# Layer 0's last MLP group added in HBM, one input combination kept in HBM, projection weights in pairs: a hybrid two-layer trunk on one Trainium2 core

## The chip, the core and the metric

The kernel runs on one core of one Trainium2 chip. Its time is the device time of one execution in microseconds (us); of the kernel before, three runs have a median of 2133.31 us (2131.84 to 2133.79). One further execution was recorded by the hardware profiler; all rows shown below come from it.

The engines are named as in the profile: PE is the matrix engine (PEld its weight loads), DVE the vector engine, ACT the scalar engine, POOL the GpSimd engine, SP the sync engine, which here only issues DMAs. L12 is line 12 of the kernel before.

## What is computed

A residual stream `x` of 1024 positions by 1024 features passes through two layers. Each layer adds a mixer and then an MLP. All data are float32.

```python
for layer in range(2):
    h = rms_norm(x, norm_mix[layer])
    if layer == 0: y_mix, xq = rglru_group(h, ...)   # gated linear recurrence
    else:          y_mix, xq = fox_group(h, ...)     # causal attention with forgetting
    y_mem = memory_group(xq, mem, ...)               # cross-attention into 256 memory tokens
    x = x + concat([y_mix, y_mem]) @ w_out[layer]
    x = x + square(relu(rms_norm(x, norm_mlp[layer]) @ w_mlp_in[layer])) @ w_mlp_out[layer]
```

`memory_group` also needs keys and values of the memory tokens: `rms_norm(mem, g_mem) @ w_kv`.

## The kernel before

The stream is held transposed in HBM (`xs`, in the trace `xspill`): eight feature blocks `m` of 128 partitions, each with 1024 positions that are worked on in two halves `h` of 512. Every float32 operand of a matmul is split into a high and a low part (`split`, `split_sb`: ACT writes the high part, DVE subtracts to get the low one), and every product is made of three matmuls (`t3`): high by high, high by low, low by high. Weights are split in the same way in `_wpart` (L316 on ACT, L317 on DVE or POOL), from four raw buffers `wr` into a ring of three `wh`/`wl` pairs. The list `plan` gives the order of the weights; `wnext` splits up to two entries ahead of the one that it returns. Raw weights are loaded by DMAs that SP issues in order (L312).

All working tiles of 128x512 are drawn from one pool of 86 slots, `F` for float32 and `R` for split parts. `get` takes the slot that was freed longest ago; the new user then waits until the last use of the old one has ended, a DMA out of it included.

**The MLP.** One Strassen-Winograd step is applied: per group `g` of eight, `mlp_z` makes the seven products of the first matrix, each of 24 matmuls of 128x512, and `mlp_out` the seven of the second. The left operands are combinations of weight blocks: for the third of a unit's seven, called S2, `_wunit` makes sums of raw blocks in place (L355 to L360), on POOL, or on DVE where the unit's `dve` is set. The right operands of `mlp_z` are five combinations of the input, `t1`, `t2`, `t3`, `t4` and `b22`, and the half 0 parts `b11` and `b21`, all split once by `xquad` and `xsplit` and held in slots for all eight groups. Each product's result goes from PSUM into slots (`copies`, L1028 on ACT; `plus`, L1033 on DVE), and in groups 0 to 6 `send` adds the sixteen finished tiles of a group into `xs` by DMAs that POOL issues with an add at the destination (L1172). In group 7 of both layers `keep` and `end` instead bring `xs` into the sums (L1192 on POOL for a quarter, by DMA with add into the tile at L1195 for a half, `acc` for the last quarter), and `sink` (L1174 on) writes the finished tile, to `xs` in layer 0 and to the output in layer 1. In layer 0 `sink` also makes the squares of every tile (L438), adds them up (L444) and splits the half 0 tiles into the next mixer's input (L468, L469).

**From layer 0 to layer 1.** `kv(1)` prepares the memory tokens (splits at L587 and L590, squares at L593, their sum at L597 on POOL) during `mlp_z` of group 7, and makes the memory's keys and values right behind the MLP; then come `norm_fin(0)`, the query projection `xq_proj(0, 1)`, the first memory attention and the forgetting attention, and `norm_split` for half 1, which loads half 1 from `xs` and splits it.

**Layer 1's MLP.** The first products of groups 0 to 3 are made early, during the mixer (`mlp_park`); group 0's four result tiles stay in slots, those of groups 1 to 3 go to HBM and are read back by `mlp_back` in the middle of `mlp_out` of the group before.

**Layer 1's output projection** uses `wout1m` and `wout1x`, each as eight entries of 512 columns, one for each output block `m`. Each set is used twice, once for each half; the second time its split parts are loaded back from HBM by POOL's DMAs (L332).

Within these functions the instructions are written out as a list; the tile framework keeps data dependences and orders each engine's instructions by a simulated schedule, so an instruction may run ahead of one that was written before it on the same engine.

Of the kernel before, what the change touches and what calls it, by code (L numbers as in the profile page):

```python
# [175 lines left out]
class Builder:  # L176
# [4 lines left out]
    def __init__(self, ctx, tc, ins, out):  # L181
# [36 lines left out]
        self.parked = {}  # L218
        self.stp = {}
# [246 lines left out]
    def split(self, xt, g, n=H):  # L466
        hi, lo = self.R.get(), self.R.get()
        self.last_hi = self.nc.scalar.activation(hi[:, :n], xt, AF.Copy, scale=g)  # L468
        self.nc.vector.scalar_tensor_tensor(lo[:, :n], xt, g, hi[:, :n].bitcast(F32), ALU.mult, ALU.subtract)  # L469
        return hi, lo  # L470
# [42 lines left out]
    def norm_split(self, h, g, src, stats):  # L513
        xs = self.xg[h] = []
        for k in range(8):
# [3 lines left out]
            xs.append(self.split(x[:, :H], self.pc(g, k)))  # L519
            self.F.put(x)  # L520
# [368 lines left out]
    def outproj(self, h, ks, src, dst, gain, last, banks=("pj",)):  # L889
        nc = self.nc  # L890
        for m in range(8):
            x = self.load_x(m, h, src)
            wh, wl = self.wnext()
            ps = self.psum(banks[m % len(banks)])
            terms = []
            for i, k in enumerate(ks):
                c = slice(i * P, (i + 1) * P)
                terms += self.t3(wh[:, c], wl[:, c], *(self.ymix[h][k] if k < 4 else self.ymem[h][k - 4]))
# [91 lines left out]
    def xsplit(self, key):  # L990
        n = slice(0, H)
        for q, f, g in self.later.pop(key, ()):
            self.tp[key][q] = self.split_sb(f[:, n]) if g is None else self.split(f[:, n], g)
            self.F.put(f)

# [6 lines left out]
    def plan_mlp(self, l, parked, wait):  # L1002
        for g in wait:
            self.plan_unit("w1", 8 * l + g, Unit.ALL[1:2])
        for g in range(8):
            u = self.plan_unit("w1", 8 * l + g, Unit.ALL[2:] if g in parked + wait else Unit.ALL)
            u.dve = g == 0
            self.plan_unit("w2", 8 * l + g)
# [64 lines left out]
    def mlp_z(self, l, g, hook):  # L1073
        nc = self.nc
        V = nc.vector
        n = slice(0, H)
        xp = dict(self.tp, b11=self.xg[0][0::2], b21=self.xg[0][1::2])
# [4 lines left out]
        def run(banks, key, start, done):  # L1082
            hook(key)
            yield from self.product(banks, xp[key], start, done)
            if g == 7:
# [67 lines left out]
    def mlp_out(self, l, g, mid):  # L1153
        nc = self.nc
        V, G = nc.vector, nc.gpsimd
        n = slice(0, H)
        hp = self.hp
        seen = set()
# [15 lines left out]

        def sink(f, q, a, b):
            x, dm = f[:, n], 2 * q + a
            nc.sync.dma_start((self.out if l else self.xs)[dm, :, b * H:(b + 1) * H], x)
            if l == 0:
                self.sqacc(1 if b in seen else 0, b, x, V if b == 0 and a == 1 else None)
                seen.add(b)  # L1180
                if b == 0:
                    self.xg[0][dm] = self.split(x, self.pc("gmix1", dm))
            self.F.put(f)

        def keep(a, b):
            dst = []

            def first(q, ps):
                self.copies(dst)(q, ps)
                if g == 7 and a == b == 0:  # L1190
                    f = self.acc.pop(0)
                    G.tensor_tensor(dst[q][:, n], dst[q][:, n], f[:, n], ALU.add)  # L1192
                    self.F.put(f)
                elif g == 7:
                    nc.gpsimd.dma_start(dst[q][:, n], self.xs[2 * q + a, :, b * H:(b + 1) * H], accum_op=ALU.add)  # L1195

            def then(q, ps):
                self.plus(dst[q], ps)
                (sink if g == 7 else send)(dst[q], q, a, b)
# [3 lines left out]
        def end(q, ps):  # L1203
            if g == 7:
# [15 lines left out]
        acc = [self.load_x(2 * q, 1, self.xs) for q in range(4)] if g == 7 else None  # L1220
# [5 lines left out]
    def mlp(self, l, wait, nxt=None):  # L1226
# [9 lines left out]
        def hook7(key):  # L1236
            if key in ("t2", "b22") and nxt is not None:
                advance(nxt)
            if key == "t1":
# [551 lines left out]
```

## Time and profile before

| what | value |
|---|---|
| median of three runs | 2133.31 us |
| profiled execution, its own time | 2132.37 us |
| profiled execution, span from first to last instruction | 2130.7 us |
| PE busy | 2071.5 us, 97% of the span, 10466 matmuls |
| DVE busy | 1663.3 us, 78% |
| ACT busy | 1141.9 us, 54% |
| POOL busy | 864.0 us, 41% |
| mean granted PE clock | 0.988 |
| moved by DMA | 298.44 MB, 140 GB/s over the span |

The MLP of layer 0 ends at about 985 us of the span and that of layer 1 at its end. In a table of windows, each row gives a stretch of the span, its length, then busy time and number of instructions of each engine, the granted PE clock (1.00 is full), the mean busy share of the 16 DMA engines and what they moved. In a list of waits a row names the waiting instruction, what released it, the total of the waits, their number and the longest. In a list of groups, a row gives line, engine, operation, tiles and shapes and the count, then the busy time in us and the mean of one instruction in ns, then the idle time of the engine ahead of it.

### The profile page before, as it was taken

How to read it: one execution, taken by the hardware profiler on the slowest of the kernel's cores; microseconds unless marked ns; L12 is line 12 of the kernel's file. 1: busy time of each engine (PE TensorE's matmuls, PEld its weight loads, DVE VectorE, ACT ScalarE, POOL GpSimd, SP SyncE). 2: the span in 40 equal slices, each digit the busy share in tenths (PEclk: the TensorE clock that was granted, in tenths of full speed). 3: DMA queues.
4: the chain of work that ended last, by engine and by line, in shares of the span. 5: the costliest groups of instructions: out<-in, count | busy, mean ns of one | idle time of the engine just before them, and what ended most of it. 6: DMA issues, size and time to landing. Idle time of an engine off the chain costs nothing. (4 is left out here: it accounts for less than half of the span.)

```text
span 2130.7 us, 30055 instructions
## 1 busy us (share of the span) xinstructions
PE 2071.5 (97%) x10466; PEld 1727.4 (81%) x10466; DVE 1663.3 (78%) x2708; ACT 1141.9 (54%) x2160; POOL 864.0 (41%) x844
## 2 busy tenths in 40 slices
PE   9999999999999999988999999999999999999998
PEld 8898878878778778767998998777777877787786
DVE  7988698877877877887677778776787768868777
ACT  6755655544454454555555646566544554445443
POOL 2222321535535525545342333422054645445444
PEclk8999999999999999989999999999999999999999
DMA  5422452546545635627768446934546675364474
GB/s 180 140 77 93 135 184 94 101 89 128 101 97 119 111 87 119 156 86 199 276 218 290 133 138 214 299 122 129 161 99 139 138 150 101 85 140 94 89 173 119
DMA packets 126392, 298.44 MB, mean 140 GB/s; under 512 B 14176, under 2 KB 16288, under 8 KB 126240
## 3 DMA queue, kind: packets, MB, share of 16 engines
q1 hardware_dynamic: 82464, 208.36, 29.4%
q0 software_dynamic: 43776, 88.17, 23.2%
q8 instruction: 82, 1.34, 0.3%
q14 instruction: 70, 0.57, 0.1%
HBM read 187.32 MB, written 109.15 MB: 139 GB/s over the span
## 5 line engine op out<-in xcount | busy, mean ns | idle before, releaser
L317 DVE TENSOR_TENSOR wl<-wr,wh 128x1024 fp32r<-128x1024 f32 (+2 forms) x362 | 441.2, 1229 | 108.5 <-ACT wh L316 104.1
L1017 PE MATMUL pspt<-r,wh 128*128 128x512 f32 x1536 | 485.1, 396 | 7.2 <-DVE r L477 2.6
L1172 POOL DMA_DIRECT2D xspill<-f x224 | 284.7, 1963 | 287.5 <-DVE f L1033 284.1
L316 ACT ACTIVATE wh<-wr 128x1024 fp32r<-128x1024 f32 (+3 forms) x411 | 306.0, 766 | 141.4 <-PE pss L1017 41.2
L1017 PEld LDWEIGHTS pspt<-r,wh 128*128 128x128 f32 x1536 | 289.0, 188 | 77.9 <-DVE r L477 4.3
L1017 PE MATMUL pss<-r,wh 128*128 128x512 f32 x1024 | 329.6, 400 | 19.8 <-ACT f L1028 8.1
L477 DVE TENSOR_TENSOR r<-f,r 128x512 fp32r<-128x512 f32 x282 | 230.1, 826 | 98.5 <-ACT r L474 39.9
L1017 PE MATMUL pspt<-r,wl 128*128 128x512 f32 x768 | 305.6, 398 | 0.2
L1017 PE MATMUL pspj<-r,wh 128*128 128x512 f32 x832 | 265.8, 399 | 2.1 <-DVE f L1033 1.0
L1017 PEld LDWEIGHTS pss<-r,wh 128*128 128x128 f32 x1024 | 192.6, 189 | 75.9 <-DVE r L477 13.9
L385 PE MATMUL pspj<-wh,r 128*128 128x256 f32 (+1 forms) x1280 | 248.5, 286 | 2.3 <-DVE r L1322 0.8
L474 ACT ACTIVATE r<-f 128x512 fp32r<-128x512 f32 x282 | 173.5, 626 | 106.2 <-DMA xspill<-f 49.0
L1038 ACT ACTIVATE f<-f 128x512 f32<-128x512 f32 x128 | 80.9, 632 | 269.5 <-DVE f L1037 269.4
L385 PEld LDWEIGHTS pspj<-wh,r 128*128 128x128 f32 x1280 | 201.6, 188 | 5.3 <-DVE r L1322 1.0
L1017 PE MATMUL pss<-r,wl 128*128 128x512 f32 x512 | 203.6, 398 | 0.0
L355 POOL TENSOR_TENSOR wr<-wr,wr 128x512 f32<-128x512 f32 x60 | 95.7, 1778 | 249.0 <-DVE wl L317 233.2
L1017 PEld LDWEIGHTS pspj<-r,wh 128*128 128x128 f32 x832 | 156.3, 189 | 39.4 <-DVE r L469 1.5
L385 PE MATMUL pspj<-wl,r 128*128 128x256 f32 (+1 forms) x640 | 181.1, 283 | 0.0
L1017 PEld LDWEIGHTS pspt<-r,wl 128*128 128x128 f32 x768 | 146.0, 190 | 36.9 <-DVE wl L317 2.0
L385 PE MATMUL pspj<-r,wh 128*128 128x512 f32 x488 | 164.1, 411 | 5.3 <-ACT r L474 2.1
L1017 PE MATMUL pspj<-r,wl 128*128 128x512 f32 x416 | 163.4, 397 | 0.6 <-DVE wl L317 0.5
L357 POOL TENSOR_TENSOR wr<-wr,f 128x512 f32<-128x512 f32 x60 | 135.4, 2550 | 17.1 <-issue 17.1
(301 smaller groups left out, 4035.3 us busy)
## 6 DMA issues: line engine op xcount, KB each, us to landing
wr<-in_w_dram SPq DMA_DIRECT2D x136, 512.0 KB, 4.5
xspill<-f POOLq DMA_DIRECT2D x224, 256.0 KB, 7.0
f<-xspill SPq DMA_DIRECT2D x88, 256.0 KB, 4.1
xspill<-f SPq DMA_DIRECT2D x64, 256.0 KB, 3.5
f<-in_xT_dram SPq DMA_DIRECT2D x32, 256.0 KB, 3.5
wr<-in_wkv_dram SPq DMA_DIRECT2D x16, 512.0 KB, 3.6
wr<-in_wina_dram SPq DMA_DIRECT2D x15, 512.0 KB, 3.6
wsp<-wh SPq DMA_DIRECT2D x14, 512.0 KB, 5.4
```

Of the source, the lines that this page charges most:

```text
L316: self.wact = self.nc.scalar.activation(hi, raw, AF.Copy)
L317: eng.tensor_tensor(lo, raw, hi.bitcast(F32), ALU.subtract)
L355: G.tensor_tensor(r["a11"][:, d], r["a11"][:, d], r["a21"][:, d], ALU.subtract)
L357: G.tensor_tensor(r["a12"][:, d], r["a12"][:, d], x, ALU.subtract)
L385: self.lastmm = self.nc.tensor.matmul(out, lhsT=a, rhs=b, start=(j == 0), stop=(j == n - 1))
L474: i = self.nc.scalar.activation(hi[:, :n], src, AF.Copy)
L477: self.nc.vector.tensor_tensor(lo[:, :n], src, hi[:, :n].bitcast(F32), ALU.subtract)
L1017: self.lastmm = self.nc.tensor.matmul(ps, lhsT=a, rhs=b, start=(start and c == 0 and j == 0), stop=(c == n - 1 and j == 2), skip_group_che ...
L1038: self.lastsq = self.nc.scalar.activation(f[:, n], f[:, n], AF.Square)
L1172: nc.gpsimd.dma_start(self.xs[2 * q + a, :, b * H:(b + 1) * H], f[:, n], accum_op=ALU.add)
```

## The change

- Group 7 of layer 0's MLP does as groups 0 to 6 do: sixteen adds into `xs` by DMA. The loads of `xs` in front of them, POOL's adds and all of `sink`'s extra work go away for layer 0; for layer 1 the first quarter's add goes from POOL to DVE, and behind the second partial sum instead of the first.
- The next mixer's half 0 is loaded from `xs` and split in `norm_split_back`, woven into the later part of `kv(1)`. Its sums of squares are made by PE (`sq_pe`, four matmuls of 128x1 a tile). For half 1 the squares are made in the later `norm_split`.
- The split `b22` is written to HBM once a layer. Its eight slots are given back after each group's `b22` product, and `b22_back` loads it again at the start of every later `mlp_z`.
- The S2 sums of the second matrix in group 7 are made on DVE and not on POOL, in both layers.
- `wout1m` and `wout1x` come as four entries of 1024 columns, each for two output blocks.

```diff
+    def norm_split_back(self, h, g, src):
+        xs = self.xg[h] = [None] * 8
+        for j, k in enumerate((0, 2, 4, 6, 1, 3, 5, 7)):
+            x = self.load_x(k, h, src)
+            xs[k] = self.split(x[:, :H], self.pc(g, k), behind=self.wact)
+            self.sq_pe(j, h, x[:, :H], self.last_hi)
+            self.F.put(x)
+            yield
...
     def outproj(self, h, ks, src, dst, gain, last, banks=("pj",)):
+        per = 8 // len(ks)
         for m in range(8):
             x = self.load_x(m, h, src)
-            wh, wl = self.wnext()
+            if m % per == 0:
+                wh, wl = self.wnext()
...
             for i, k in enumerate(ks):
+                i += m % per * len(ks)
...
     def xsplit(self, key):
...
+            if key == "b22":
+                d = self.b22[q] = [self.dr.tile([P, H], F32R, name=self.nm("xsp")) for _ in range(2)]
+                for a, b in zip(d, self.tp[key][q]):
+                    self.nc.sync.dma_start(a.bitcast(F32), b.bitcast(F32))
+
+    def b22_back(self):
+        for q in range(4):
+            self.tp["b22"][q] = self.R.get(), self.R.get()
+            for a, b in zip(self.tp["b22"][q], self.b22[q]):
+                self.nc.sync.dma_start(a.bitcast(F32), b.bitcast(F32))
...
-            self.plan_unit("w2", 8 * l + g)
+            u = self.plan_unit("w2", 8 * l + g)
+            u.dve = g == 7
...
     # mlp_z
+        if g:
+            self.b22_back()
...
-            if g == 7:
+            if g == 7 or key == "b22":
                 for a, b in xp[key]:
                     self.R.put(a, b)
...
     # mlp_out
+        last = l == 1 and g == 7
+
         def sink(f, q, a, b):
-            x, dm = f[:, n], 2 * q + a
-            nc.sync.dma_start((self.out if l else self.xs)[dm, :, b * H:(b + 1) * H], x)
-            if l == 0:
-                self.sqacc(1 if b in seen else 0, b, x, V if b == 0 and a == 1 else None)
-                seen.add(b)
-                if b == 0:
-                    self.xg[0][dm] = self.split(x, self.pc("gmix1", dm))
+            nc.sync.dma_start(self.out[2 * q + a, :, b * H:(b + 1) * H], f[:, n])
             self.F.put(f)
...
             def first(q, ps):
                 self.copies(dst)(q, ps)
-                if g == 7 and a == b == 0:
-                    f = self.acc.pop(0)
-                    G.tensor_tensor(dst[q][:, n], dst[q][:, n], f[:, n], ALU.add)
-                    self.F.put(f)
-                elif g == 7:
+                if last and (a or b):
                     nc.gpsimd.dma_start(dst[q][:, n], self.xs[2 * q + a, :, b * H:(b + 1) * H], accum_op=ALU.add)
 
             def then(q, ps):
                 self.plus(dst[q], ps)
-                (sink if g == 7 else send)(dst[q], q, a, b)
+                if last and not (a or b):
+                    f = self.acc.pop(0)
+                    V.tensor_tensor(dst[q][:, n], dst[q][:, n], f[:, n], ALU.add)
+                    self.F.put(f)
+                (sink if last else send)(dst[q], q, a, b)
...
-        self.plan += [self.ent("wout1m", m, 512, 1) for m in range(8)]
+        self.plan += [self.ent("wout1m", m, 1024, 1) for m in range(4)]
...
     # run
-        advance(kv, 5)
+        advance(kv, 6)
+        weave(kv, self.norm_split_back(0, "gmix1", self.xs), 1.0)
+        self.vst = {}
+        xq = self.xq_proj(0, 1)
+        advance(xq, 4)
         self.norm_fin(0, False, self.lastmm)
-        drain(kv)
-        self.vst = {}
-        drain(self.xq_proj(0, 1))
-        self.norm_fin(1, False)
+        drain(xq)
...
-        weave(self.fox_proj(0, 1), self.norm_split(1, "gmix1", self.xs, False), 0.5)
+        weave(self.fox_proj(0, 1), self.norm_split(1, "gmix1", self.xs, True), 0.5)
+        self.norm_fin(1, False)
```

More of the change, by code (lines that the diff above doesn't have):

```diff
@@ L218, in __init__ @@
         self.parked = {}
+        self.b22 = [None] * 4
         self.stp = {}
@@ L464, in sq_mm, with split @@
             self.F.put(sq)
-    def split(self, xt, g, n=H):
+    def split(self, xt, g, n=H, behind=None):
         hi, lo = self.R.get(), self.R.get()
         self.last_hi = self.nc.scalar.activation(hi[:, :n], xt, AF.Copy, scale=g)
+        if behind is not None:
+            self.after(self.last_hi, behind)
         self.nc.vector.scalar_tensor_tensor(lo[:, :n], xt, g, hi[:, :n].bitcast(F32), ALU.mult, ALU.subtract)
@@ L1154, in mlp_out @@
         nc = self.nc
-        V, G = nc.vector, nc.gpsimd
+        V = nc.vector
         n = slice(0, H)
         hp = self.hp
-        seen = set()
         def run(banks, key, start, done, ahead=None):
@@ L1198, in then @@
                 self.plus(dst[q], ps)
-                (sink if g == 7 else send)(dst[q], q, a, b)
+                if last and not (a or b):
[3 more added lines that the diff above has]
+                (sink if last else send)(dst[q], q, a, b)
             return first, then
         def end(q, ps):
-            if g == 7:
+            if last:
                 self.plus(acc[q], ps)
@@ L1219, in mlp_out @@
         C = [self.psum(k) for k in more]
-        acc = [self.load_x(2 * q, 1, self.xs) for q in range(4)] if g == 7 else None
+        acc = [self.load_x(2 * q, 1, self.xs) for q in range(4)] if last else None
         yield from run(C, "t3", True, c22[0], "t4")
@@ L1238, in hook7 @@
                 advance(nxt)
-            if key == "t1":
+            if key == "t1" and l:
                 self.acc = [self.load_x(2 * q, 0, self.xs) for q in range(4)]
@@ L1254, in mlp @@
                     self.pool_parts = TUNE["pb0"]
-                    self.xg[0] = [None] * 8
             drain(self.mlp_out(l, g, lambda: self.mlp_back(g + 1)))
@@ L1537, in run @@
         self.plan_fox(1)
-        self.plan += [self.ent("wout1x", m, 512, 1) for m in range(8)]
-        self.plan += [self.ent("wout1m", m, 512, 1) for m in range(8)]
+        self.plan += [self.ent("wout1x", m, 1024, 1) for m in range(4)]
+        self.plan += [self.ent("wout1m", m, 1024, 1) for m in range(4)]
         for g in TUNE["park"]:
@@ L1543, in run @@
             self.plan_unit("w1", 8 + g, Unit.ALL[:1])
-        self.plan += [self.ent("wout1x", m, 512, 1) for m in range(8)]
+        self.plan += [self.ent("wout1x", m, 1024, 1) for m in range(4)]
         self.plan_mlp(1, TUNE["park"], TUNE["wait"])
@@ L1732, in _pack @@
         o[nme] = st(C(w[ks].reshape(-1, D)))
+        if len(ks) == 4:
+            o[nme] = C(o[nme].reshape(4, 2, P, 512).transpose(0, 2, 1, 3).reshape(4, P, 1024))
     w1, w2 = [], []
```

## The prediction

> **What bounds the kernel now.** I read the page first, then a table of windows over the stages.
>
> ```profile
> span 2130.7 us, 30055 instructions
> PE 2071.5 (97%) x10466; PEld 1727.4 (81%) x10466; DVE 1663.3 (78%) x2708; ACT 1141.9 (54%) x2160; POOL 864.0 (41%) x844
> ```
>
> PE is the bound: 2130.7 − 2071.5 leaves 59.2 us without a matmul. The change takes no large matmul away, so it can only win idle PE time, and time in which PE's clock is low. The windows show where both lie (length, PE busy, PEld, DVE, ACT, POOL, granted clock, DMA share, GB/s):
>
> ```profile
> 300.00:925.00 625.00, 622.83 (x2695) 500.56 (x2694) 491.80 (x555) 311.84 (x493) 265.80 (x221) 1.00 0.51 111
> 925.00:980.00 55.00, 44.29 (x167) 32.86 (x165) 45.84 (x50) 31.61 (x59) 33.01 (x27) 0.88 0.41 105
> 980.00:1005.00 25.00, 19.64 (x112) 17.79 (x113) 23.90 (x42) 16.58 (x39) 17.48 (x15) 0.88 0.76 235
> 1480.00:1500.00 20.00, 16.38 (x71) 13.39 (x70) 10.55 (x19) 7.40 (x13) 4.29 (x8) 0.83 0.65 189
> 1560.00:1740.00 180.00, 171.16 (x717) 135.74 (x716) 136.15 (x150) 88.43 (x143) 97.17 (x80) 0.98 0.61 132
> 2070.00:2105.00 35.00, 31.36 (x126) 24.26 (x125) 34.22 (x36) 17.73 (x29) 19.61 (x11) 0.95 0.03 12
> ```
>
> Layer 0's groups before the last are full (2.2 us idle in 625). Four places are not: the end of layer 0 (55 − 44.29 = 10.7 and 25 − 19.64 = 5.4, together 16.1 us), the last part of layer 1's projection (3.6), layer 1's groups 0 to 2 (8.8) and its group 7 (3.6). Behind the stalls the clock is low; the same view over those stretches alone, for PE (length, busy, clock, DMA share, GB/s):
>
> ```profile
> 944.10:957.90 13.80, 8.75 (x19) 0.51 0.28 96
> 1490.10:1497.80 7.70, 7.64 (x28) 0.56 0.98 308
> 1566.80:1572.10 5.30, 5.27 (x12) 0.50 0.61 143
> ```
>
> Busy time by (1 − clock) is what this costs: 8.75 × 0.49 = 4.3, 7.64 × 0.44 = 3.4 and 5.27 × 0.50 = 2.6 us. So the places hold 20.4, 7.0, 11.4 and 3.6 us, 42 us in all, and the change touches each of them.
>
> **The end of layer 0.** Its groups of instructions from 921.8 to 964, POOL's and then DVE's (busy us, mean ns):
>
> ```profile
> L1192 POOL TENSOR_TENSOR f<-f,f 128x512 f32<-128x512 f32 x4 | 6.3, 1600 | 0.7 <-ACT f L1028 0.7
> L444 POOL TENSOR_TENSOR f<-f,f 128x512 f32<-128x512 f32 x3 | 5.0, 1674 | 12.0 <-ACT f L438 12.0
> L597 POOL TENSOR_TENSOR f<-f,f 128x512 f32<-128x512 f32 x3 | 4.2, 1391 | 0.2
> L355 POOL TENSOR_TENSOR wr<-wr,wr 128x512 f32<-128x512 f32 x2 | 3.0, 1516 | 17.3 <-DVE wl L317 17.3
> L356 POOL TENSOR_TENSOR f<-wr,wr 128x512 f32<-128x512 f32 x2 | 3.0, 1519 | 0.0
> L360 POOL TENSOR_TENSOR wr<-wr,wr 128x1024 f32<-128x1024 f32 x1 | 2.9, 2854 | 0.0
> L357 POOL TENSOR_TENSOR wr<-wr,f 128x512 f32<-128x512 f32 x2 | 2.7, 1386 | 1.2 <-issue 1.2
> ```
>
> ```profile
> L477 DVE TENSOR_TENSOR r<-f,r 128x512 fp32r<-128x512 f32 x10 | 12.1, 1221 | 0.0
> L590 DVE SCALAR_TENSOR_TENSOR r<-f,par,r 128x256 fp32r<-128x256 f32 x8 | 8.6, 1135 | 0.0
> L317 DVE TENSOR_TENSOR wl<-wr,wh 128x1024 fp32r<-128x1024 f32 x3 | 5.8, 1948 | 0.0
> ```
>
> Beside these, DVE's groups from 1470 to 1520, where POOL reads little:
>
> ```profile
> L477 DVE TENSOR_TENSOR r<-f,r 128x512 fp32r<-128x512 f32 x10 | 6.9, 686 | 2.0 <-ACT r L474 1.9
> ...
> L360 DVE TENSOR_TENSOR wr<-wr,wr 128x1024 f32<-128x1024 f32 x1 | 1.2, 1218 | 0.0
> L1459 DVE TENSOR_TENSOR r<-pspt,r 128x256 fp32r<-128x256 f32 x2 | 0.8, 412 | 0.0
> ```
>
> The reader is to see that DVE is slowed while POOL computes. The excess is 10 × (1221 − 686) = 5.4 us, 8 × (1135 − 412) = 5.8 and 3 × (1948 − 1218) = 2.2, 13.4 us in these three groups. POOL is busy there for 27.1 us, of which the change leaves only L597's 4.2, about a sixth; so some 11 us of the excess go. Against that DVE takes over S2's sums: six at 0.69 as L477 and one at 1.22, 5.4 us. DVE also loses the first four of eight half 0 splits here (they come later). Net it is some 6 to 9 us less busy in a stretch in which PE idled 10.7 us for it. I leave 3 us of stall, since the memory token splits L590 still stand in front of group 7's own chain. Two waits come further on:
>
> ```profile
> PE pspt L385 <- DVE wl L317: 3.7, 2, 2.6
> ```
>
> ```profile
> DVE f L1033 <- DMA f<-xspill: 7.3, 2, 6.7
> ```
>
> DVE's 7.3 us wait is for `xs` brought into the sums by DMA, which layer 0 no longer does: the sixteen sums leave by DMA, behind nothing that PE needs. L317 was late because `sink`'s squares, adds and splits shared ACT and DVE with the weights. The eight loads, splits and squares now come within the second half of the memory projection, so I leave 3 us here too. The place keeps 6 of 20.4 us: **−14.4**. Bounds: it keeps nothing, or all 20.4.
>
> What the new path itself needs is covered. These rows give an add into `xs`, a load of it, and a load's issue (min/median/max ns):
>
> ```profile
> xspill<-f POOLq DMA_DIRECT2D x224, 256.0 KB, 7.0
> f<-xspill SPq DMA_DIRECT2D x88, 256.0 KB, 4.1
> ```
>
> ```profile
> L510 SPq DMA_DIRECT2D f<-xspill x88: 319/326/1971, 234.1 to 2063.1; - x88
> ```
>
> The last half 0 sum is made by the product before the last, about 24 matmuls ahead of the MLP's end, which is some 5 us; 7.0 + 4.1 us and two splits later (about 1.4 us) it is ready, some 8 us after that end. The eight memory products of 24 matmuls stand between the end and the query projection that reads it. If ACT's in-order queue reached a split before its load had landed, the weights' L316 behind it would be late, and PE with it: that is in the bound of 20.4 kept.
>
> PE gets 28 more small matmuls (32 by `sq_pe` in place of 4). L462's row in the window view, 300 to 925:
>
> ```profile
> 300.00:925.00 625.00, 7.57 (x64) 8.37 (x64) 1.00 0.51 111
> ```
>
> 7.57 / 64 = 0.118 us each, so **+3.3**. The squares for half 1 move to ACT and POOL in the attention stage, where PE does not wait for either: 0.
>
> **Layer 1's groups 0 to 2.** PE's waits and ACT's from 1560 to 1740:
>
> ```profile
> PE pss L1017 <- ACT f L1028: 8.1, 3, 3.9
> ```
>
> ```profile
> ACT f L1028 <- DMA xspill<-f: 9.5, 3, 5.3
> ...
> ACT f L1028 <- DVE wl L317: 2.4, 1, 2.4
> ```
>
> All three stalls are one thing: ACT wants to empty a PSUM bank, and its slot is not free yet, because an add DMA still reads it or DVE still uses it. By the code, 58 of 86 slots are held through the MLP (16 for half 0, 40 for the five combinations, 2 for the scales). At the start of `mlp_out` 20 of the other 28 hold group results, which leaves 8, and groups 0 to 2 give 4 of them to the parked tiles. The change hands `mlp_out` the 8 of `b22`: more than the parked tiles take, so these groups have at least the room that groups 4 to 6 have, which do not stall. 2 of 11.4 us kept: **−9.4**; bounds, nothing gained or all 11.4.
>
> **The projection.** Of the 3.6 us idle, the second of these is the change's:
>
> ```profile
> PE pspj L385 <- ACT r L474: 2.1, 1, 2.1
> PE pspj L385 <- DMA wh<-wsp: 1.0, 1, 1.0
> ```
>
> With entries for two blocks the ring holds weights for six, so the third entry is asked for four blocks ahead of its use. I take the 1.0 and half of the slow clock: **−2.7**, bounds 0 and −7.0. Fewer and larger splits save ACT and DVE time in stages where PE does not wait: 0.
>
> **Layer 1's group 7.** It has the same S2 sums and L1192:
>
> ```profile
> L1192 POOL TENSOR_TENSOR f<-f,f 128x512 f32<-128x512 f32 x4 | 6.5, 1632 | 5.7 <-ACT f L1028 5.7
> ```
>
> ```profile
> L477 DVE TENSOR_TENSOR r<-f,r 128x512 fp32r<-128x512 f32 x12 | 14.2, 1197 | 0.0
> ```
>
> L477 alone is slowed by 12 × (1197 − 686) = 6.1 us, and nearly nothing of POOL's reading stays. DVE takes 5.4 for the sums and 4 × 0.69 = 2.8 for the adds, the latter after PE's wait. PE waits on L477, so I take **−2.5** of 3.6; bounds, 3.6 won or 5.4 lost, if the sums land ahead of that chain and the relief does not.
>
> **The reload of `b22`.** Seven times a layer SP issues eight loads, 8 × 0.326 = 2.6 us. What stands behind them on SP are raw weights, and those are early:
>
> ```profile
> SPq L312 <- DVE wl L317: 532.3, 66, 28.3
> ```
>
> Over layer 0's groups SP stands for 532 us waiting for a weight buffer to be emptied, not for a DMA. `b22` itself is used five or seven products later, over 20 us (24 matmuls at 0.233 each, from 625 us by 2695). So its cost is next to nothing: I take **+2**, for queueing with the adds. Bounds: 0, and 14 × 2.6 = +37 with all issue time on the path.
>
> [...]
>
> The sum: −14.4 + 3.3 − 9.4 − 2.7 − 2.5 + 2 = −23.7 us. The profiled execution took 2132.4 us (1.7 more than its span) and the median is 0.9 above it, so 2133.3 − 23.7 = 2109.6, which I round to 2110.
>
> [...]
>
> **The rivals.**
>
> 1. *The forecast*, 2110: 58 in 100. Its own range is 2096 to 2121, the end of layer 0 and group 7 being the loose terms.
> 2. *DVE stays the bound at the end of layer 0.* S2's sums enter DVE's queue ahead of group 7's chain, and the splits and squares meet the memory weights instead. For it: DVE is at 45.84 of 55 and 23.90 of 25 us. Against it: the 11 us of excess. Without the 14.4: 2124. 12 in 100.
> 3. *The freed slots do not help*, because the order in which slots come round puts the waits elsewhere. For it: the stalls follow the landing of adds, 7.0 us. Against it: stalls only where four slots fewer are free. Without the 9.4: 2119. 10 in 100. With case 2 as well: 2133, no change, 7 in 100.
> 4. *The reload holds up the weights.* SP is in order; if in each group the eight loads stand ahead of raw blocks that are due, each of 14 reloads costs its 2.6 us, +37 in place of +2: 2145. It decides from 25.7 / 14 = 1.8 us a reload on. Against it: the 532 us. 13 in 100.
>
> **How the numbers follow.** Something like 0.2%, 4 us, can be told from no change. Cases 1, 2, 3 are faster: 0.58 + 0.12 + 0.10 = 0.80; both failing is the same, 0.07; case 4 slower, 0.13. From 2096 to 2134 holds all but case 4 and the forecast's own tails.
>
> **What would show it.** From 925 to 1005 idle PE near 6 us instead of 16 and no long stretch at half clock; L477 and L590 near 0.7 and 0.5 us there. From the start of layer 1's MLP no L1028 waiting for an add. In group 7 no L355 to L360 on POOL. L462 at 224 instead of 192. I am wrong if PE waits for `b22`, if L316 waits for raw weights at the head of groups, or if ACT stands for the reloaded `xs` while the memory weights wait behind it.

## The result: 0.6% slower, and the profile after

The changed kernel took 2146.47 us (median of four runs, 2144.92 to 2147.10) where the kernel before took 2133.55 beside it: ratio 1.006, 95% interval 1.0042 to 1.0077, so 9 to 16 us slower. The prediction was 2110, with 2096 to 2134 as its range; the time is 36 us above the one and 12 above the end of the other. One execution among the runs below, of the kernel with its projection weights in eight entries, took 11.5 ms and is left out of that run's figures.

The head of the page after:

```profile
span 2145.4 us, 30330 instructions
PE 2079.9 (97%) x10522; PEld 1733.0 (81%) x10522; DVE 1636.3 (76%) x2710; ACT 1143.5 (53%) x2156; POOL 822.4 (38%) x811
```

PE stays the bound. It is busy 8.4 us longer than before (2071.5), although the product matmuls are the same, and idle for 65.5 us in place of 59.2. For where, both traces are cut at the same matmuls: a stage reaches from the first product matmul of one group to that of the next, and the second mixer with layer 0's last stalls lies between the two MLPs. Lengths in us, worked out from the matmuls' start times of one profiled execution each:

| stage | before | after | difference |
|---|---|---|---|
| layer 0, groups 0 to 6 | 555.1 | 567.3 | +12.2 |
| layer 0, group 7 | 96.6 | 84.6 | −12.0 |
| second mixer | 531.7 | 542.9 | +11.2 |
| layer 1, group 0 | 78.0 | 81.9 | +3.9 |
| layer 1, groups 1 and 2 | 140.9 | 134.8 | −6.1 |
| layer 1, groups 3 to 6 | 304.3 | 313.9 | +9.6 |
| layer 1, group 7 | 88.1 | 83.1 | −5.0 |

The stretch ahead of the first group, which no edit here is aimed at, took 335.7 to 338.6 us in the profiles, so a difference of 2 or 3 us in one stage may be chance.

Three places won: both groups 7 (layer 0's about as predicted, layer 1's twice as much), and layer 1's groups 1 and 2. The losses stand in the groups that had no stall, in the mixer, and in layer 1's group 0. The window view after, in the places of the prediction's table (length, PE busy, PEld, DVE, ACT, POOL, clock, DMA share, GB/s):

```profile
300.00:935.00 635.00, 624.06 (x2685) 497.78 (x2684) 489.46 (x554) 312.16 (x494) 264.40 (x218) 1.00 0.56 135
926.00:980.00 54.00, 49.94 (x206) 39.22 (x205) 45.06 (x65) 31.89 (x57) 14.67 (x15) 0.97 0.34 81
980.00:1012.00 32.00, 31.11 (x225) 28.96 (x223) 18.85 (x52) 18.09 (x47) 17.47 (x22) 1.00 0.93 245
1613.00:1748.00 135.00, 134.89 (x579) 108.36 (x578) 100.40 (x116) 68.05 (x111) 74.58 (x60) 1.00 0.68 170
2088.00:2125.00 37.00, 37.00 (x161) 29.98 (x160) 34.38 (x52) 22.97 (x38) 4.32 (x6) 1.00 0.14 39
```

At the end of layer 0 PE idles 4.1 us of 54, at clock 0.97 where it was 0.88, and 0.9 of the next 32: 5.0 in all, near the 6 that the prediction gave as a sign. In groups 1 and 2 of layer 1 it idles 0.1 of 135. In layer 1's group 0 the old stall (L1028, 3.9 us) is gone and a longer one stands in its place (of PE's waits from 1510 to 1615):

```profile
PE pss L1043 <- DVE r L480: 5.8, 1, 5.8
```

But the first row of the windows, the groups that were full (2.2 us idle of 625), now has 10.9 idle of 635. What changed at the end of layer 0 is seen in DVE's groups from 922 to 968:

```profile
L480 DVE TENSOR_TENSOR r<-f,r 128x512 fp32r<-128x512 f32 x12 | 7.8, 678 | 0.0
L318 DVE TENSOR_TENSOR wl<-wr,wh 128x1024 fp32r<-128x1024 f32 x6 | 7.3, 1217 | 5.1 <-ACT wh L317 5.1
L602 DVE SCALAR_TENSOR_TENSOR r<-f,par,r 128x256 fp32r<-128x256 f32 x8 | 6.5, 858 | 0.0
```

The splits that took 1221 ns beside POOL's sums take 678, L317's former 1948 are 1217. The memory token splits (L602, before L590) fall from 1135 to 858 ns only, not to the 0.5 us given as a sign.

Where the full groups lose is in the waits from 400 to 900 us (`pss`, `pspj`, `pspt` and `pso` are banks of PSUM). Before:

```profile
ACT r L474 <- DMA xspill<-f: 25.1, 7, 4.3
PE pss L1017 <- DVE r L477: 1.5, 6, 0.3
PE pspj L1017 <- DVE wl L317: 0.5, 1, 0.5
```

After:

```profile
ACT r L477 <- DMA xspill<-f: 53.2, 7, 9.1
PE pspj L1043 <- ACT f L1054: 5.4, 6, 1.6
PE pspt L1043 <- DVE wl L318: 2.4, 6, 0.4
PE pspt L1043 <- ACT f L1054: 1.7, 1, 1.7
PE pspj L1043 <- DVE wl L318: 1.4, 1, 1.4
```

ACT waited 25 us in seven places for a slot that an add was still reading, and PE hardly felt it. Now ACT waits 53, and PE waits 7.1 us for the bank copies (L1054) behind it and 3.8 for split weights (L318; 0.5 before). The sync engine, the price of rival 4, is not it. Its waits from 480 to 900:

```profile
SPq L313 <- DVE wl L318: 233.0, 43, 19.5
SPq L1019 <- DVE r L480: 144.8, 11, 27.4
```

It still stands for weight buffers to be emptied (393.5 us before, now 233) and beside that for `b22`'s slots. ACT's waits for raw weights in the same groups hardly moved (18.4 us in four places before, 21.1 in five after, from 400 to 900).

### The profile page after: what moved, and what is told of

Same layout as the page of the kernel before. It is cut to its first block, busy times and chain, and to the rows that moved or that the text cites. A ratio compares the mean times of both kernels' runs of the same rounds, so it can differ in the third digit from the quotient of the medians.

```text
span 2145.4 us, 30330 instructions
## 1 busy us (share of the span) xinstructions
PE 2079.9 (97%) x10522; PEld 1733.0 (81%) x10522; DVE 1636.3 (76%) x2710; ACT 1143.5 (53%) x2156; POOL 822.4 (38%) x811
## 5 line engine op out<-in xcount | busy, mean ns | idle before, releaser
L318 DVE TENSOR_TENSOR wl<-wr,wh 128x1024 fp32r<-128x1024 f32 (+2 forms) x354 | 431.2, 1228 | 203.7 <-ACT wh L317 194.2
L1199 POOL DMA_DIRECT2D xspill<-f x240 | 304.5, 1990 | 332.3 <-DVE f L1059 325.3
L317 ACT ACTIVATE wh<-wr 128x1024 fp32r<-128x1024 f32 (+3 forms) x403 | 303.7, 777 | 144.7 <-DMA wr<-in_w_dram 34.5
L1043 PE MATMUL pspj<-r,wh 128*128 128x512 f32 x832 | 272.7, 402 | 13.6 <-ACT f L1054 11.1
L480 DVE TENSOR_TENSOR r<-f,r 128x512 fp32r<-128x512 f32 x282 | 218.2, 787 | 31.8 <-ACT r L477 25.6
L1043 PEld LDWEIGHTS pss<-r,wh 128*128 128x128 f32 x1024 | 192.0, 188 | 58.2 <-DVE r L480 10.9
L356 POOL TENSOR_TENSOR wr<-wr,wr 128x512 f32<-128x512 f32 x56 | 90.2, 1806 | 220.4 <-DVE wl L318 200.8
L386 PE MATMUL pspj<-r,wh 128*128 128x512 f32 x488 | 161.7, 407 | 6.6 <-ACT r L469 1.9
L358 POOL TENSOR_TENSOR wr<-wr,f 128x512 f32<-128x512 f32 x56 | 134.9, 2765 | 15.8 <-issue 15.8
```

Of the source, the lines that this page charges most:

```text
L317: self.wact = self.nc.scalar.activation(hi, raw, AF.Copy)
L318: eng.tensor_tensor(lo, raw, hi.bitcast(F32), ALU.subtract)
L356: G.tensor_tensor(r["a11"][:, d], r["a11"][:, d], r["a21"][:, d], ALU.subtract)
L358: G.tensor_tensor(r["a12"][:, d], r["a12"][:, d], x, ALU.subtract)
L386: self.lastmm = self.nc.tensor.matmul(out, lhsT=a, rhs=b, start=(j == 0), stop=(j == n - 1))
L480: self.nc.vector.tensor_tensor(lo[:, :n], src, hi[:, :n].bitcast(F32), ALU.subtract)
```

## The experiments

Each ratio, with its 95% interval, is to the kernel before, timed on the same chip beside it. Between chips the kernel before differs (medians of 2132.0 to 2135.4 us), so runs on different chips are compared by their ratios. A profile is one execution, up to 4 us away from its run's median. The first four runs start from the changed kernel.

**`b22` stays in its slots.** `b22_back` and the stores left out, and the slots freed in group 7 alone:

```diff
-            if g == 7 or key == "b22":
+            if g == 7:
```

> The kernel after with b22 kept in its eight slots (no store, no reload, slots held through the MLP as before). Theory A (the reload's DMAs stand beside each group's first four adds, so these land 2 to 3 us later and ACT waits for their slots): layer 0's groups 0 to 6 go back to about 79 us each (12 us) and layer 1's groups 3 to 6 too (9.5 us), layer 1's groups 1 and 2 lose the 6 us they had won: about 2131. Theory B (the loss comes from the other parts, the reload being free): 2146, no change.

Measured: 2132.27 us, 0.999 [0.9973, 1.0008]. Layer 0's groups 0 to 6 are back at 555.2. So the round trip as a whole costs (1.006 − 0.999) × 2133, about 15 us, net of what the slots win in layer 1. The intervals do not overlap.

**The reload later.** It is written ahead of the fifth product, behind the last raw load, when no add of the first four is under way; the slots go round as changed:

```diff
-        if g:
-            self.b22_back()
...
+        if g:
+            self.b22_back(self.lastraw)
         yield from run(A, "t1", False, c22)
```

> The kernel after with the reload written ahead of the fifth of mlp_z's seven products and queued on SP behind the last weight load written before it. Slots are given back as in the kernel after, and as many bytes are moved, but away from the adds. Theory A: the first four adds of a group land in 4 to 5 us again, the groups take 79 us, about 2126. Rival (the issue of eight loads on SP holds up the weights, wherever it stands): 2146 or more, L317 waiting for raw weights. Rival (handing the slots round is what hurts): 2146.

Measured: 2145.95 us, 1.0061 [1.0038, 1.0084]. The reload now runs some 10 to 24 us into a group, away from the first four adds. The profile shows layer 0's groups 0 to 6 at 561.3, half of the loss gone, and the win of layer 1's groups 1 and 2 nearly gone as well (139.6). It is of the fastest of four executions (2142.81).

**The traffic alone.** The reload goes into the same slots, which are never given back:

```diff
-            self.tp["b22"][q] = self.R.get(), self.R.get()
             for a, b in zip(self.tp["b22"][q], self.b22[q]):
...
-            if g == 7 or key == "b22":
+            if g == 7:
```

> The kernel after with the reload into the same eight slots: stored and loaded again in every group, but the slots are never given to others. Theory A: the traffic alone costs, layer 0's groups stay at 80 to 82 us and layer 1's groups 1 and 2 lose what they had won, 2146 to 2156. Rival (the changed round of slots costs, not the traffic): as without the reload, about 2131.

Measured: 2135.19 us, 1.0007 [0.9994, 1.002]; full groups take 78.8. The reload's 112 reads of 256 KB, 29 MB, cost 3.6 us by the middle values (1.0007 against 0.999), and the intervals overlap. This does not test theory A, though. The reload waits here only for the last use of the old `b22`: in group 3 its eight reads go out at 37.0 to 40.2 us and have landed by 47, ahead of the group's first add at 52.6. In the changed kernel six of the eight go out between 52.3 and 61.5 us, beside the first four adds. What the run does show is that the bytes and their issue on SP cost little in themselves, and that with the slots kept the first add goes out at 52.6 us, as in the kernel before, and not at 54.4 as in the changed one.

**The weights in eight entries.** The changed kernel with the projection's entries of 512 columns again:

```diff
-        self.plan += [self.ent("wout1m", m, 1024, 1) for m in range(4)]
+        self.plan += [self.ent("wout1m", m, 512, 1) for m in range(8)]
...
```

> The kernel after with layer 1's projection weights in eight entries of 512 columns again. If the pairs cause the loss in the mixer stage (543 us after, 532 before, of which 3.3 are the 28 small matmuls): about 2139. If that loss comes from the squares of half 1 and the later norm, or from another order of instructions: 2146.

Measured: 2140.01 us, 1.0028 [1.0016, 1.004]. By the ratios the pairs cost 6.8 us of the changed kernel's time. A run with the pairs alone follows further down.

### What the slots do

By these runs the traffic is not the whole cost: with the slots going round, moving it away from the first adds mends only half of layer 0's loss. The order of DVE's instructions shows what else the giving back of the slots changed. DVE's timeline before, from the first bank of `b22`'s product in layer 0's group 3 (L1037) to the first partial sum (start, us, line):

```profile
619.97 0.68 DVE L1037 SCALAR_TENSOR_TENSOR f<-pspt,f 128x512 f32<-128x512 f32 x1
...
623.58 0.68 DVE L477 TENSOR_TENSOR r<-f,r 128x512 fp32r<-128x512 f32 x1
...
625.99 0.68 DVE L477 TENSOR_TENSOR r<-f,r 128x512 fp32r<-128x512 f32 x1
626.59 0.68 DVE L1033 TENSOR_TENSOR f<-f,pspt 128x512 f32<-128x512 f32 x1
```

After, in the same group:

```profile
627.80 0.68 DVE L1063 SCALAR_TENSOR_TENSOR f<-pspt,f 128x512 f32<-128x512 f32 x1
...
630.21 0.68 DVE L480 TENSOR_TENSOR r<-f,r 128x512 fp32r<-128x512 f32 x1
...
632.01 1.29 DVE L480 TENSOR_TENSOR r<-f,r 128x512 fp32r<-128x512 f32 x2
...
634.42 1.28 DVE L480 TENSOR_TENSOR r<-f,r 128x512 fp32r<-128x512 f32 x2
...
636.23 0.68 DVE L1059 TENSOR_TENSOR f<-f,pspt 128x512 f32<-128x512 f32 x1
```

Five splits stand there in place of two. The planned order pulls three more splits ahead of the first sum; 8.43 − 6.62 = 1.81 us is three of them. That it can do so because free slots need not be waited for is argued; that it goes with the giving back of the slots is shown by the runs that keep them. The sum goes out later, and so does its add. On ACT the same group then shows the last split pulled ahead, in a slot that an add drains, with the fourth bank copy of the product behind it:

```profile
640.50 0.60 ACT L1054 ACTIVATE f<-pspj 128x512 f32<-128x512 f32 x1
648.12 0.63 ACT L477 ACTIVATE r<-f 128x512 fp32r<-128x512 f32 x1 [7.01 <-DMA xspill<-f]
648.66 1.04 ACT L317 ACTIVATE wh<-wr 128x1024 fp32r<-128x1024 f32 x1
649.60 0.58 ACT L1054 ACTIVATE f<-pspj 128x512 f32<-128x512 f32 x1
```

The end of the wait, 648.12, is the landing of the group's third add. That gives a test of four corners, sums early or late and traffic beside the adds or not.

**Sums early, traffic beside.** The splits of `t3` and `t1` are tied behind the first sums of the group:

```diff
-                    hp[ahead].append(self.split_sb(f[:, n]))
+                    hp[ahead].append(self.split_sb(f[:, n], pin=self.lastplus if ahead in ("t3", "t1") else None))
```

(`pin` puts DVE's half of the split behind that sum, and `t3`'s splits are written behind the first bank's sum. So the edit also moves ACT's half of `t3`'s splits; late sums and ACT's own order are not told apart.)

> The changed kernel, b22's trip and the slots given back as they are, but in the output half of each group the splits of t3 and t1 are tied behind the first sums, so that VectorE makes three splits ahead of the first sum, as in the kernel before, where the changed kernel makes six. Theory H (the free slots let the schedule pull splits ahead of the sums; the sums and their adds go out 1.8 us later, and the last split, which takes a slot that an add drains, holds up ScalarE with the next bank copy behind it): the first add is issued at 52.6 us of the group again in place of 54.4, a full group falls from 80 to 81.5 us to 78.8 to 79.8, ScalarE's wait for adds between 400 and 900 us from 53 to about 30, and the time from 2146.5 to 2132 to 2138. Theory A (the reload beside the adds, or its issue on the sync engine): no change, 2145 to 2147.

Measured: 2150.87 us, 1.0065 [1.0044, 1.0086]. The first add went out at 52.6 us again, as expected, and the time did not fall: theory H by itself fails, and theory A's "no change" holds within the interval. With the reload beside them the adds land later, the third 6.7 us after its issue where it was 4.5.

**Sums early, no traffic beside.** Both edits.

> The changed kernel with both: the splits of t3 and t1 tied behind the first sums, and the reload written ahead of the fifth product, so that it moves while no add does. Slots are still given back and taken again. Each alone left the third add of a group landing 2.4 to 2.8 us later than before (offset 61.2 us in the kernel before, 65.1 changed, 63.7 with the late reload, 64.0 with the tied splits), and the last split ahead, with bank copies behind it, waits for that add. Theory HA (late sums and traffic each carry half of it, and either half is enough to make TensorE wait): the third add lands near 61.5, a full group falls to 78.8 to 79.2 us, and the time to 2132 to 2137. Theory S (whatever the adds do, a split too many ahead is what blocks; ScalarE has 9 in place of 7 splits ahead of the second product's first copy): groups stay at 80 to 82 and the time at 2143 to 2150.

Measured: 2130.49 us, 0.9979 [0.997, 0.9989]. The table has the four corners, the kernel before and the run with the traffic alone; the adds are those of layer 0's group 3, in us from its first product matmul:

| sums, traffic | third add issued | takes | landed | groups 0 to 6 |
|---|---|---|---|---|
| kernel before | 56.7 | 4.5 | 61.2 | 555.1 |
| slots kept, traffic at 37 to 47 us | 56.7 | 4.4 | 61.1 | 554.6 |
| changed (late, beside) | 57.9 | 7.2 | 65.1 | 567.3 |
| late, no traffic | 57.9 | 5.4 | 63.3 | 561.3 |
| early, beside | 57.3 | 6.7 | 64.0 | 571.8 |
| early, no traffic | 57.3 | 4.8 | 62.1 | 556.1 |

PE's longest kind of wait from 400 to 900 with sums early and traffic beside, and then with neither fault:

```profile
PE pss L1045 <- ACT f L1056: 11.0, 6, 2.0
```

```profile
PE pspj L1045 <- ACT f L1056: 1.4, 1, 1.4
```

So where the third add landed at 61 to 62 us the groups were full, and where it landed at 63 or later they were not. Either fault alone costs 6 to 17 us in these groups, and only with both mended is the loss gone: theory HA holds, with "late sums" read as the whole order that the pin changes, and S fails. The landings are read from one group, the lengths from all seven. The waits for split weights go with early sums too (0.4 us left). The landing does not set the size of the loss: early sums with the traffic beside land at 64.0 and cost more (571.8) than late sums at 65.1 (567.3). PE then waits for another bank's copy, `pss` where it was mostly `pspj`. ACT's wait for adds alone would have misled: it is 42.6 us in the mended kernel, whose groups are full, and 42.3 with the reload later, where 6 us are lost. What counts is what stands behind a wait and when it ends. Even so the mended kernel is not told apart from the one that keeps the slots (0.999 [0.9973, 1.0008]): its layer 1 wins less in groups 1 and 2 (138.3) and still loses in group 3 (70.7, before 68.0).

On ACT the trace shows the copy at 649.60 taken only behind the split that waited: it comes 9.1 us after the copy before it, with 7.01 of it the split's wait. The third add takes 4.8 us with the reload elsewhere and 6.7 with the reload beside it (sums early in both); in what way the one slows the other is not seen in these runs.

### The end of layer 0, the pairs and the mixer

**Without `b22`'s trip and pairs.**

> The changed kernel with b22 kept in its slots and the projection's weights in eight entries of 512 again: what is left is the end of layer 0 (the sums added in HBM, the next mixer's input read back, 28 small matmuls for the sums of squares) and S2 of the two last groups on VectorE. From the stages of the runs so far: layer 0's last group -12, layer 1's last group -5, the mixer +6.5 (its +9.5 without b22's trip less the 3 that the eight entries gave back), layer 1's first group +2.5, in all about -8: 2126 us, 2123 to 2129. If the pairs cost something only together with b22's trip: 2132, as with the trip alone taken out. If the reading back at the start of the mixer costs more than the profile of one execution shows: 2130 or above.

Measured: 2130.63 us, 0.997 [0.9957, 0.9984]; the end of layer 0 and S2 win 0.3%, 6.4 us by the ratio (4.8 by the medians on this chip, where the kernel before took 2135.41), less than the 8 expected. The time falls into the expectation's last case, 2130 or above. The mixer takes 543.8 in the profile although no pairs are in it; that execution was the slowest of the eight (2133.68).

**The same, S2 back on GpSimd** (`u.dve = g == 7` left out).

> The run before this one, with S2 of the last groups' output weights back on GpSimd. If S2 on VectorE is what shortened layer 1's last group (88.1 us before, 83.1 after, its products waiting for weights), that group goes back to 87 to 88 us and layer 0's last group grows by 2 to 4: 2131 to 2135 us in all, 5 to 9 above the run before. If the shortening came from the sums and their order alone, both groups stay and the time is within 2 us of the run before.

Measured: 2137.08 us, 1.0004 [0.9992, 1.0016], 7 us above the run before, of which the groups 7 show 4.4: layer 0's goes from 84.9 to 87.7, layer 1's from 82.2 to 83.8, not to 87. So of the 11.7 and 5.9 us that they won over the kernel before, S2 on VectorE is 2.8 and 1.6. The rest came with the other edits to the two groups, the adds, loads and squares taken out or moved, which no run separates. DVE's splits from 922 to 968, without S2 on GpSimd and with it, show that GpSimd's sums slow them:

```profile
L480 DVE TENSOR_TENSOR r<-f,r 128x512 fp32r<-128x512 f32 x11 | 7.2, 680 | 0.0
```

```profile
L480 DVE TENSOR_TENSOR r<-f,r 128x512 fp32r<-128x512 f32 x11 | 10.3, 950 | 0.0
```

**The kernel before with pairs alone** (the entries and the loop's one fetch for two blocks).

> The kernel before with only the last projection's weights in pairs. If the pairs cost by themselves what the changed kernel gained without them: the mixer 3 us longer and the whole 2137 to 2140 us. If they cost only behind the reordered norm (weights and the read-back input at the same time): 2133 to 2135. By the prediction's -2.7 us: 2131.

Measured: 2142.67 us, 1.0031 [1.0018, 1.0044]: the pairs cost 6.6 us by themselves, the mixer 3.5 and layer 1's group 0 another 3.1. PE's waits for stored weights from 980 to 1540, before and with pairs, are

```profile
PE pspj L385 <- DMA wh<-wsp: 1.0, 1, 1.0
```

```profile
PE pspj L385 <- DMA wh<-wsp: 3.6, 3, 1.8
```

The one wait that the pairs were to take away became three.

**Reads at the mixer's start.** The kernel before with eight reads of half 0, unused:

```diff
-        drain(kv)
+        weave(kv, reads(), 1.0)
```

> The kernel before with eight reads of half 0 (2 MB) woven into the keys and values of the second mixer, as the changed kernel reads its input there; nothing uses what they bring, beyond one column each. Theory D (the mixer's start is carried by the DMA engines, at 0.9 of their time from 1120 to 1160 us, and 2 MB at the 330 GB/s reached there are 6 us, which the last projection's stored weights then come late by): mixer 531.7 to 535 to 538, waits for those weights from 1 to 4 us, 2136 to 2140 in all. If the reads are hidden: within 2 us of the kernel before.

Measured: 2134.39 us, 1.0003 [0.9993, 1.0013], mixer 531.6. Theory D fails, the reads are hidden.

**`b22`'s trip only where it won.** Entries of 512, slots given back in layer 1's groups 0 to 2:

```diff
-            if g == 7 or key == "b22":
+            if g == 7 or (l and g <= 2 and key == "b22"):
```

> The end of layer 0 and S2 as changed, the projection's weights in eight entries, and b22's trip only where it gained: its slots are given back in layer 1's groups 0 to 2 and taken again in groups 1 to 3; in layer 0 and from group 3 on it stays. From the stages: the kernel without the trip and without pairs (2130.6) less 4 to 7 in layer 1's groups 1 and 2 (70 to 72 us each there, 67.4 with the slots), groups 3 to 6 at 68 and 78.8: 2125 us, 2122 to 2128. If the trip costs what it gains at group 3, as in the changed kernel (72.0 for 68.0): 2129 to 2131.

Measured: 2125.03 us, 0.9955 [0.994, 0.997], as expected. Groups 1 and 2 take 135.2 where they took 144.1 without the trip, and group 3, which gives no slot back, 67.8 as before. The interval overlaps that of the run without the trip (0.997), so the gain rests on the stage.

**Half 1's squares early.** On top of that:

```diff
-        drain(xq)
+
+        def squares():
+            for k in range(8):
+                x = self.load_x(k, 1, self.xs)
+                self.sqacc(k, 1, x[:, :H])
+                self.F.put(x)
+                yield
+
+        sq = squares()
+        weave(xq, sq, 2.0)
+        drain(sq)
+        self.norm_fin(1, False)
...
-        weave(self.fox_proj(0, 1), self.norm_split(1, "gmix1", self.xs, True), 0.5)
-        self.norm_fin(1, False)
+        weave(self.fox_proj(0, 1), self.norm_split(1, "gmix1", self.xs, False), 0.5)
```

> The run of the trip kept to layer 1's first groups, with the squares of half 1 taken back to where their sum was ready before: eight extra reads of half 1 and its squares beside the queries of half 0, its norm finished right behind them, none of it in the forget-attention stage. Theory N (the norm of half 1, finished at 1133 to 1140 us inside the first output projection in place of 1045, and its eight squares and sums, are what the mixer lost between 1115 and 1260 us): the mixer falls from 542 to 534 to 538 and the time from 2125 to 2117 to 2121. Theory P (the 32 small matmuls and the reading back at the mixer's start are what it lost): no gain, 2124 to 2128.

Measured: 2118.96 us, 0.9931 [0.9913, 0.9949]: the fastest version that computes everything, 0.7% under the kernel before. The gain of some 5 us over the run before (by the ratios, whose intervals overlap) is the expected one, but not where it was expected: the profile has the mixer at 542.2, unchanged, and layer 1's group 0 at 78.4 in place of 82.3.

**The kernel before, its norm late.** The opposite move, made in the kernel before and nothing else:

```diff
             if l == 0:
-                self.sqacc(1 if b in seen else 0, b, x, V if b == 0 and a == 1 else None)
+                if b == 0:
+                    self.sqacc(1 if b in seen else 0, b, x, V if a == 1 else None)
...
-        self.norm_fin(1, False)
...
-        weave(self.fox_proj(0, 1), self.norm_split(1, "gmix1", self.xs, False), 0.5)
+        weave(self.fox_proj(0, 1), self.norm_split(1, "gmix1", self.xs, True), 0.5)
+        self.norm_fin(1, False)
```

> The kernel before, with only half 1's squares and norm moved to where the changed kernel has them: no squares of half 1 at the end of layer 0, but on the blocks read back in the forget-attention stage, and its norm finished behind that stage. Theory N (this move alone costs 4 to 5 us, between 1115 us and the first group of layer 1): 2136 to 2139, and nothing else changes; eight squares and sums less at layer 0's end give back 1 to 2 of it at most. If it costs only together with the reading back of half 0: 2131 to 2134.

Measured: 2137.86 us, 1.002 [1.001, 1.0029], 4 us slower: theory N holds in size. In the profile the mixer takes 535.9. PE's waits from 1090 to 1260 with this move alone (the kernel before has 1.9 us there in all, none over 0.5):

```profile
PE pss L1414 <- DVE mn L1419: 2.6, 2, 1.9
PE pspj L385 <- DVE f L558: 1.3, 1, 1.3
PE pspj L385 <- DVE xnb L700: 1.3, 1, 1.3
PE pspj L385 <- DMA wl<-wsp: 0.8, 1, 0.8
PE pspj L385 <- DMA wh<-wsp: 0.6, 1, 0.6
PE pso L1447 <- DVE r L1460: 0.6, 2, 0.5
```

**Half 0's squares on GpSimd** (`sqacc` for `sq_pe`, on the version with the trip only where it won).

> The same base with the squares of half 0 summed on GpSimd, as the kernel before did it, in place of TensorE's 32 small matmuls (64 records, 7.7 us busy, where the kernel before had 16 records, 2.9). Theory P: the mixer falls by 4 to 6 us, 2119 to 2122. Theory N: the matmuls stand where TensorE waits for its input anyway, and GpSimd's last sum comes later: no gain or a loss, 2125 to 2130.

Measured: 2140.80 us, 1.0036 [1.0023, 1.0049], 15 us slower than its base. This tells the two theories not apart, since a new stall came: from 1000 to 1040 PE is busy 22.3 of 40 us at clock 0.57, waiting for splits,

```profile
PE pspj L386 <- ACT r L469: 12.2, 4, 3.9
```

and the splits wait for blocks to be read (ACT L469, 20.9 us). Why these come later was not tried.

**24 of the 32 small matmuls left out**, on the fastest version.

> The run with half 1's squares early (2119.0 us), with 24 of half 0's 32 small matmuls left out (those of six of its eight row blocks; the norm of half 0 is then wrong by that). They are 48 records of 0.12 us each. Theory P2 (they stand on TensorE's path, TensorE being the bound at the mixer's start): 5 to 6 us less, 2113 to 2114.5. If they lie in time in which TensorE would wait for the reading back anyway: 2118 to 2120.

Measured: 2114.14 us, 0.9908 [0.9893, 0.9923], 4.8 us less than with them (4.9 by the ratios, whose intervals overlap). The mixer falls from 542.2 to 537.5 in the profiles, and no other stage moves by more than 0.4: they are on PE's path. The rows of the small matmuls from 980 to 1160 (from 970 in the last) before, after, and with 24 left out:

```profile
L378 PE MATMUL pso<-cD,f 128*128 128x1 f32 x16 | 2.9, 292 | 0.3 <-DVE f L444 0.3
```

```profile
L463 PE MATMUL pso<-cD,f 128*128 128x1 f32 x64 | 7.7, 244 | 1.5 <-ACT f L450 1.5
```

```profile
L465 PE MATMUL pso<-cD,f 128*128 128x1 f32 x16 | 2.2, 256 | 0.0
```

32 matmuls make 64 records: each of these f32 matmuls of one column shows as two.

## Why the prediction was wrong

Step by step; "measured" is a run's time or ratio where there is one, otherwise the stages of the one profile. The terms come from different runs and each may be 2 or 3 us off, so that their sum comes near the whole proves little.

| step | predicted | measured |
|---|---|---|
| end of layer 0 | −14.4 | −12.0 (group 7's stage) |
| 28 small matmuls | +3.3 | +5.6 (28 × 4.8 / 24) |
| half 1's squares moved | 0 | +4.0 (by themselves), 5 (taken back) |
| layer 1, groups 0 to 2 | −9.4 | −6.1 (groups 1 and 2) |
| the projection's pairs | −2.7 | +6.6 (by themselves), 6.8 (taken back) |
| layer 1, group 7 | −2.5 | −5.0 (stage) |
| `b22`'s reload | +2 | +21.8 (stages: 12.2 and 9.6) |
| sum | −23.7 | +14.9, against 13 in all |

- *The end of layer 0* came near in size, and clock and splits recovered. That POOL's sums had slowed DVE is shown for S2 (680 against 950 ns, 2.8 us of the stage); what the other edits carry is not separated. The excess of L590 was worked out from another operation of the same size (L1459, 412 ns) and was too large: 858 ns are left of 1135.
- *The reload of `b22`* is the step that failed, and with it the sign. It was priced at SP's issue time, which costs little (1.0007 with the same loads into kept slots, 0.9979 with the slots going round and both faults mended), and at 2 us for queueing with the adds, the author's estimate, for which no row was given. It cost 21.8, and its bounds, 0 to +37, held that by luck, since they were worked out from SP's issue time. Two things were left out. The eight slots, counted as a win for layer 1's groups 0 to 2, were given back in the other groups too, which had no stall to lose; there the order of DVE and ACT changed and the sums came late, which alone costs 6.2 us of layer 0's 12.2. And the reload came to stand beside the first adds, which alone (sums early) costs 16.7: the adds land later, and what ACT has queued behind them, PE waits for. Rival 3 named "the order in which slots come round" but gave it a price of no gain, never a loss. Rival 4 had the time (2145) by coincidence, with weights held up on SP, which did not happen. (625 us by 2695 matmuls is 0.232 us each, not 0.233, which changes nothing.)
- *Layer 1's groups 0 to 2*: groups 1 and 2 lost their stalls whole. Group 0 was counted with them and lost 3.9: its old stall (L1028, 3.9 us) is gone, but PE waits 5.8 us there for a split of DVE, which the prediction did not foresee.
- *The small matmuls* were mis-sized: 0.118 us is the price of a record, and 64 records were taken for 64 matmuls where they are 32. L463 stands at 256 records, not at the 224 given as a sign.
- *The squares of half 1* were called free because PE waits for neither ACT nor POOL there. What is late next is the norm behind them, finished inside the first output projection, where PE then waits for DVE and for stored weights; that the late norm brings these waits is argued from their place.
- *The pairs*: the one quoted wait of 1.0 us was to go. A wait for the same weights came three times instead. That a fetch for two blocks asks for twice as much at once is argued, not shown.
- *Layer 1's group 7* won twice the predicted amount, more than the 3.6 us of idle time that bounded it. The place was read too narrowly (2070 to 2105; the stage has 7.4 us idle before and 4.8 after), and its low clock was left out: 31.36 us busy at 0.95 lose 1.6 us by the prediction's own measure, and after the change the clock is 1.00.

What stays open: even with the norm early the mixer takes 542 us in its profile, 5 more than the small matmuls explain (that execution, 2122.01, was the slowest of four and 3 above the median). At 1120 to 1140 PE is busy only 15.8 of 20 us there, at clock 0.86, and waits 2.2 and 1.5 us for the attention's queries (ACT L1398, DVE L1400); why these are late was not tried. With the traffic alone the mixer took 549 us in its profile, 8 more than with the slots simply kept, although the edit lies outside it; mixer lengths of single profiles are weak evidence. Layer 1's group 0 takes 77.9 to 78.7 us in six profiles and 80.2 to 82.5 in the other eleven. Every kernel with pairs is among the long ones, but without pairs some are long and some short, and the one with half 0's squares on GpSimd is short (78.1) with its norm late, so neither the pairs nor the norm alone decide it.

## What to carry to other kernels

A freed buffer is not free: it changes what an ahead-of-time order can pull forward, also in the stages that had no stall, so free it only where a stall was seen (here in layer 1's first groups: 0.9955 of the time before, where it is 0.997 with nothing freed, with overlapping intervals). Price a wait by what stands behind it on its engine (here a bank copy, 9.1 us after the one before it) and by when it ends, not by its length; and when two faults each suffice to cause a stall, mending one may win nothing in all (1.0061 and 1.0065 here, from 1.006). When work is moved "off the path", look for who consumes its result, not for who runs it.

## What the runs showed of the hardware

- One f32 matmul of one column shows as two records, 250 ns each by the median and 0.12 us of busy time, so 32 of them took 7.7 us, and leaving 24 out took 4.8 off the time.
- The reload's 112 reads of 256 KB, 29 MB, cost little or nothing where they ran 37 to 47 us into a group, ahead of its first adds (1.0007, 0.9994 to 1.002, against 0.999 without them), and 2 MB at the mixer's start cost nothing that can be told (1.0003). Beside the accumulating DMAs the same reads lengthened the third of these from 4.8 to 6.7 us (sums early in both; these times are read from layer 0's group 3).
- DVE's split of 128x512 took 1221 ns by the mean where GpSimd made its sums and 678 where they were gone; with S2's sums alone back on GpSimd it took 950, against 680.
